# Score product of a neighbourhood attention: one strided matmul or two contiguous ones

## The chip, the cores and the metric

The kernel runs on 1 core of one Trainium2 chip. The metric is the device time of one execution in microseconds (us); the median of the runs is compared. The engines are named as in the profile: PE is the tensor engine's matmul, PEld its weight load, DVE the vector engine, ACT the scalar engine, POOL GpSimd, SP the engine that issues most transfers.

## What is computed

Two layers of a diffusion backbone over 512 latent tokens (a grid of 8 rows and 64 columns) and 256 context tokens, with 1024 features. Layer 1 mixes tokens in two ways, side by side: C, a neighbourhood attention with 8 heads of 64, and D, a bidirectional RWKV-7 recurrence. The change touches C alone:

```python
def neighborhood_attention(q, k, v, kc, vc, rpb):
    ...
    def block(args):
        ...
        s_loc = jnp.einsum('bchd,bicjhd->bhcij', q_row, ks, ...) * SCALE + bias
        s_ctx = jnp.einsum('bchd,bnhd->bhcn', q_row, kc, ...) * SCALE
        s = jnp.concatenate([s_loc.reshape(B, H, GRID_W, n_loc), s_ctx], axis=-1)
        p = jax.nn.softmax(s, axis=-1).astype(v.dtype)
        ...
        return (jnp.einsum('bhcij,bicjhd->bchd', p_loc, vs)
                + jnp.einsum('bhcn,bnhd->bchd', p[..., n_loc:], vc))
```

Every query sees a window of latent keys (8 rows by 16 columns) with a bias, and all 256 context keys, under one softmax.

## The kernel before, in words

The latent tokens of C are stored column by column of the grid (8 tokens to a column), so the window of 128 queries lies within 256 neighbouring keys. The heads are worked in 4 pairs (`odd_pair`), each pair in 4 blocks of 128 queries, each block once for each of the two heads u: 32 calls of the inner `attend(i, b, u, sums)`. One call takes a bank of PSUM `s` (tile `ps_a`, two buffers) of 128 queries by 512 keys: 256 near keys, which begin at token `START[b]`, and the 256 context keys. In the key tile `kt` (`ck` in the profile) each head has 768 columns, 512 latent ones and then the context. The near keys and the context are therefore two runs of 256 columns, at a distance of `NX - START[b]`. For block 3, whose near keys start at 256, that distance is 256, and the two runs are one.

Float32 precision of the scores is made with two products, j = 0 and 1: queries and keys are split into a high and a low part, stacked over the partitions, and the two matmuls (weights `qt[:, j, u, ...]`, tile `cq`) add up in PSUM. This is L1043, 64 matmuls in all. Then DVE adds the bias and takes the maximum (L1048, which reads the whole bank), ACT takes the exponential (L1049), four transposes (L1055) and their copy (L1057) follow, and the value product (L633) of the block after that; a division by the sums (L618, L622, L626) ends a pair.

These steps are generators laid piecewise among the steps of D's scan over the latent chunks (`rwkv_step`: matmuls L1307, L1313, L1326, L1336 and L1345, with 32 or 64 rows or columns of the array, copies L1317, L1329 and L1347, state updates L1337, L1340 and L1341), L3 = 1.7 pieces beside each. Beyond that, a scheduler sets the order on every engine, one instruction at a time, by priority and by when its operands are expected. Score products are written under `tc.high_priority(offset=QK_AHEAD)` with QK_AHEAD = 30, so they are placed ahead of what is written before them. Each engine then runs its own list in order, and waits on semaphores for the others.

## Time and profile before

| | |
|---|---|
| Median of 3 runs | 2101.39 us (2100.31 to 2101.66) |
| Span of the profiled execution | 2097.7 us, first to last instruction |
| Median less that span | 3.7 us |
| PE busy | 1990.2 us, 95% of the span, 15774 matmuls |
| DVE, ACT, POOL busy | 1229.5, 893.1, 232.8 us |
| Mean granted PE clock | 0.969 |
| Score matmuls L1043 | 64, from 1524.2 to 1648.6 us |

The profile is of one execution; its own time beside the span is not listed, so the span is held against the median of the runs. A row of a group reads: line, engine, operation, the tile written, the tiles read, shapes, count. In the order of time a row has the start, the length and the count of what was merged. A matmul in 32-bit float of the scan or of the value product stands with two records for each instruction; a score matmul and a transpose stand with one.

### The profile page before, as it was taken

How to read it: one execution, taken by the hardware profiler on the slowest of the kernel's cores; microseconds unless marked ns; L12 is line 12 of the kernel's file. 1: busy time of each engine (PE TensorE's matmuls, PEld its weight loads, DVE VectorE, ACT ScalarE, POOL GpSimd, SP SyncE). 2: the span in 40 equal slices, each digit the busy share in tenths (PEclk: the TensorE clock that was granted, in tenths of full speed). 3: DMA queues.
4: the chain of work that ended last, by engine and by line, in shares of the span. 5: the costliest groups of instructions: out<-in, count | busy, mean ns of one | idle time of the engine just before them, and what ended most of it. 6: DMA issues, size and time to landing. Idle time of an engine off the chain costs nothing.

```text
span 2097.7 us, 38650 instructions
## 1 busy us (share of the span) xinstructions
PE 1990.2 (95%) x15774; PEld 1619.9 (77%) x15774; DVE 1229.5 (59%) x2407; ACT 893.1 (43%) x1682; POOL 232.8 (11%) x346
## 2 busy tenths in 40 slices
PE   6999999999998999999999999889899989999997
PEld 4766788999987888787777776667667778888887
DVE  5756677666666443558445656786766774333335
ACT  3335567676733433552222345535245443222222
POOL 1111100000000010000112132322222120000000
PEclk9999999999999999999999899989789999999999
DMA  7363322433484444433434323356765133232321
GB/s 271 116 207 122 142 92 81 141 131 122 138 278 150 150 156 155 134 109 102 139 111 132 111 71 91 115 160 174 169 208 142 33 121 100 92 101 90 100 92 49
DMA packets 112656, 272.68 MB, mean 130 GB/s; under 512 B 15424, under 2 KB 48736, under 8 KB 110944
## 3 DMA queue, kind: packets, MB, share of 16 engines
q1 hardware_dynamic: 100256, 224.74, 33.8%
q0 software_dynamic: 12224, 45.49, 6.6%
q8 instruction: 124, 2.03, 0.4%
q14 instruction: 52, 0.43, 0.1%
HBM read 238.20 MB, written 31.98 MB: 129 GB/s over the span
## 4 chain that ended last, share of the span: by engine, by line
PE 46%; DVE 9%; issue 2%; ACT 2%; POOL 0%; DMA 0%; DVEq 0%; ACTq 0%
PE ps_b L385 10%; PE ps_b L386 10%; PE ps_b L387 10%; PE ps_w L1307 2%; PE ps_w L1313 1%; PE ps_s L1336 1%; DVE pi L1255 1%; PE ps_w L1326 1%; DVE kb L1251 1%; DVE kb L1258 1%; PE ps_a L1043 1%; PE ps_e L1214 1%; PE ps_w L1345 1%; PE ps_e L1055 1%; PE ps_v L633 1%
## 5 line engine op out<-in xcount | busy, mean ns | idle before, releaser
L143 ACT CAST whi<-wraw 128x1024 fp32r<-128x1024 f32 (+2 forms) x291 | 293.0, 1008 | 677.1 <-PE ps_b L386 513.7
L145 DVE TENSOR_TENSOR wlo<-wraw,whi 128x1024 fp32r<-128x1024 f32 (+2 forms) x251 | 296.4, 1181 | 217.8 <-ACT whi L143 211.2
L385 PE MATMUL ps_b<-hxh,whi 128*128 128x512 f32 (+1 forms) x1040 | 402.6, 390 | 13.2 <-ACT cj L974 7.2
L386 PE MATMUL ps_b<-hxl,whi 128*128 128x512 f32 (+1 forms) x1040 | 399.3, 386 | 0.8 <-DVE hxl L378 0.6
L387 PE MATMUL ps_b<-hxh,wlo 128*128 128x512 f32 (+1 forms) x1040 | 398.2, 385 | 0.8 <-POOL wlo L145 0.5
L385 PEld LDWEIGHTS ps_b<-hxh,whi 128*128 128x128 f32 x1040 | 199.0, 193 | 61.9 <-ACT cj L974 7.8
L386 PEld LDWEIGHTS ps_b<-hxl,whi 128*128 128x128 f32 x1040 | 199.7, 193 | 39.8 <-DVE hxl L378 2.2
L387 PEld LDWEIGHTS ps_b<-hxh,wlo 128*128 128x128 f32 x1040 | 199.6, 193 | 39.4 <-DVE wlo L145 1.4
L385 PE MATMUL ps_b<-act,whi 128*128 128x512 f32 (+1 forms) x570 | 199.9, 351 | 4.8 <-DVE xx L418 2.1
L387 PE MATMUL ps_b<-act,wlo 128*128 128x512 f32 (+1 forms) x570 | 196.6, 345 | 1.5 <-DVE wlo L145 1.5
L386 PE MATMUL ps_b<-act,whi 128*128 128x512 f32 (+1 forms) x570 | 196.0, 344 | 0.6 <-DVE act L124 0.6
L385 PE MATMUL ps_b<-hch,whi 128*128 128x256 f32 x552 | 159.4, 289 | 0.1
L387 PE MATMUL ps_b<-hch,wlo 128*128 128x256 f32 x552 | 155.8, 283 | 0.2 <-DVE wlo L145 0.2
L386 PE MATMUL ps_b<-hcl,whi 128*128 128x256 f32 x552 | 155.5, 282 | 0.0
L385 PEld LDWEIGHTS ps_b<-act,whi 128*128 128x128 f32 x570 | 109.0, 191 | 22.9 <-issue 6.8
L387 PEld LDWEIGHTS ps_b<-act,wlo 128*128 128x128 f32 x570 | 109.0, 191 | 14.9 <-DVE wlo L145 2.1
L386 PEld LDWEIGHTS ps_b<-act,whi 128*128 128x128 f32 x570 | 109.0, 191 | 12.9 <-DVE act L124 1.0
L418 DVE SCALAR_TENSOR_TENSOR xx<-ps_b,mod,xx 128x512 f32<-128x512 f32 (+1 forms) x64 | 43.7, 683 | 124.1 <-PE ps_b L387 123.5
L145 POOL TENSOR_TENSOR wlo<-wraw,whi 128x1024 fp32r<-128x1024 f32 (+1 forms) x40 | 88.2, 2212 | 205.4 <-ACT whi L143 198.6
L709 DVE TENSOR_TENSOR ff_a<-ff_a,ps_b 128x512 f32<-128x512 f32 x44 | 30.2, 686 | 134.5 <-PE ps_b L387 133.8
L385 PEld LDWEIGHTS ps_b<-hch,whi 128*128 128x128 f32 x552 | 104.1, 189 | 6.3 <-issue 2.6
L387 PEld LDWEIGHTS ps_b<-hch,wlo 128*128 128x128 f32 x552 | 104.1, 189 | 1.5 <-DVE wlo L145 1.0
(369 smaller groups left out, 3471.6 us busy)
## 6 DMA issues: line engine op xcount, KB each, us to landing
wraw<-in_ffi SPq DMA_DIRECT2D x132, 512.0 KB, 3.5
xx<-in_wmod POOLq DMA_DIRECT2D x48, 512.0 KB, 5.2
wraw<-in_w1in SPq DMA_DIRECT2D x43, 512.0 KB, 3.5
wraw<-in_ffo SPq DMA_DIRECT2D x48, 448.0 KB, 3.3
wmod<-in_wmod POOLq DMA_DIRECT2D x32, 512.0 KB, 4.7
wraw<-in_ffo SPq DMA_DIRECT2D x24, 512.0 KB, 3.5
op<-op SPq DMA_DIRECT2D x32, 384.0 KB, 3.9
qx<-in_wmod SPq DMA_DIRECT2D x16, 512.0 KB, 6.2
```

The source lines that it names most:

```text
L143: self.nc.scalar.copy(hi[:, 0:n], raw)
L145: e.tensor_tensor(lo[:, 0:n], raw, hi[:, 0:n].bitcast(F32), op=ALU.subtract)
L385: mm(out, lhsT=wh, rhs=hh, start=first, stop=False)
L386: mm(out, lhsT=wh, rhs=hl, start=False, stop=False)
L387: mm(out, lhsT=wl, rhs=hh, start=False, stop=last)
L418: self.nc.vector.scalar_tensor_tensor(X[:, m, c], ps[:, 0:n][:, c], gate[:, m, i : i + 1], X[:, m, c], op0=ALU.mult, op1=ALU.add)
L633: self.nc.tensor.matmul(ps[HD * u : HD * u + HD, col : col + P], lhsT=vs[u][j], rhs=pts[u][:, j, :], start=j == 0, stop=j == nk - 1, tile_ ...
L709: V.tensor_tensor(a, a, pg[1][:, 0:w], op=ALU.mult)
L1043: nc.tensor.matmul(s, lhsT=qt[:, j, u, P * b : P * b + P], rhs=k, start=j == 0, stop=j == 1)
L1055: nc.tensor.transpose(pt[:, P * j : P * j + P], p[:, P * j : P * j + P], self.ident)
L1214: nc.tensor.matmul(pg[r, c, 0:W], lhsT=KB[r, c, :], rhs=AR[r, c, :], start=True, stop=True)
L1307: mm(wy[HD * u + HD - W_ + r : HD * u + HD, p, :], lhsT=G[top[u], p, r:W_], rhs=VU[top[u], p, u, :], start=p == 0, stop=False, skip_group_ ...
```

## The change

The one matmul of 512 columns with a stride between two runs becomes two of 256 contiguous columns, near and context, each summed over j on its own half of the bank. The order of writing is near j = 0, near j = 1, context j = 0, context j = 1. All else that differs between the two files is comments and docstrings; lines below move by two (L1048 is L1050 in the changed kernel, L1307 is L1309, and so on).

```diff
         def attend(i, b, u, sums):
             s = self.bank("a")
-            c, d = NT * u + START[b], NX - START[b]
-            k = kt[:, c : c + 2 * d].rearrange("p (a n) -> p a n", a=2)[:, :, 0:256]
+            near, ctx = (kt[:, c : c + 256] for c in (NT * u + START[b], NT * u + NX))
             with self.tc.high_priority(offset=QK_AHEAD):
-                for j in range(2):
-                    nc.tensor.matmul(s, lhsT=qt[:, j, u, P * b : P * b + P], rhs=k, start=j == 0, stop=j == 1)
+                for i, k in enumerate((near, ctx)):
+                    for j in range(2):
+                        nc.tensor.matmul(
+                            s[:, 256 * i : 256 * i + 256], lhsT=qt[:, j, u, P * b : P * b + P], rhs=k, start=j == 0, stop=j == 1
+                        )
             v = (1, 0, 0, 2)[b]
```

PE's order in the scan step beside the second pair of heads, query block 2, head 1 (`ps_a_16316`), before. `ps_w` is the scan's PSUM, `VU`, `op` and `Sd` its operands:

```order
L1313 MATMUL ps_w_16263<-Sd_1521_7227,op_2809_16044 64x64 x8
L1043 MATMUL ps_a_16316<-ck_15848,cq_15847 128x512
L1307 MATMUL ps_w_16282<-VU_1527_7237,op_2810_16048 64x64
L1043 MATMUL ps_a_16316<-ck_15848,cq_15847 128x512
L1307 MATMUL ps_w_16282<-VU_1527_7237,op_2810_16048 64x64
L1307 MATMUL ps_w_16282<-VU_1527_7237,op_2810_16048 32x64 x6
L1313 MATMUL ps_w_16282<-Sd_1525_7235,op_2810_16048 64x64 x8
```

The score product breaks into the scan's L1307 at two places. The same place in the changed kernel:

```order
L1315 MATMUL ps_w_16289<-Sd_1521_7227,op_2809_16060 64x64 x8
L1043 MATMUL ps_a_16342<-ck_15858,cq_15857 128x256
L1309 MATMUL ps_w_16308<-VU_1527_7237,op_2810_16064 64x64
L1043 MATMUL ps_a_16342<-ck_15858,cq_15857 128x256
L1309 MATMUL ps_w_16308<-VU_1527_7237,op_2810_16064 64x64
L1043 MATMUL ps_a_16342<-ck_15858,cq_15857 128x256
L1309 MATMUL ps_w_16308<-VU_1527_7237,op_2810_16064 32x64
L1043 MATMUL ps_a_16342<-ck_15858,cq_15857 128x256
L1309 MATMUL ps_w_16308<-VU_1527_7237,op_2810_16064 32x64 x5
L1315 MATMUL ps_w_16308<-Sd_1525_7235,op_2810_16064 64x64 x8
```

Now there are four places, with a scan matmul between each two. A little later, PE's order around the last block of the same pair (block 3, head 1, `ps_a_16372`), before:

```order
L1326 MATMUL ps_w_16263<-W_16280,op_2809_16044 32x64 x8
L1043 MATMUL ps_a_16372<-ck_15848,cq_15847 128x512
L1326 MATMUL ps_w_16282<-W_16299,op_2810_16048 32x64
L1043 MATMUL ps_a_16372<-ck_15848,cq_15847 128x512
L1326 MATMUL ps_w_16282<-W_16299,op_2810_16048 32x64 x7
```

There the second matmul follows one scan matmul after the first. The same place in the changed kernel:

```order
L1328 MATMUL ps_w_16308<-W_16325,op_2810_16064 32x64
L1043 MATMUL ps_a_16402<-ck_15858,cq_15857 128x256
L1328 MATMUL ps_w_16308<-W_16325,op_2810_16064 32x64
L1043 MATMUL ps_a_16402<-ck_15858,cq_15857 128x256
L1328 MATMUL ps_w_16308<-W_16325,op_2810_16064 32x64
L1043 MATMUL ps_a_16402<-ck_15858,cq_15857 128x256
L1328 MATMUL ps_w_16308<-W_16325,op_2810_16064 32x64
L1043 MATMUL ps_a_16402<-ck_15858,cq_15857 128x256
L1328 MATMUL ps_w_16308<-W_16325,op_2810_16064 32x64 x4
```

Again four single matmuls take the place of two. Over the whole program the score matmuls stand in 50 uninterrupted runs before, and in 81 after.

## The prediction

> **What bounds the kernel now.** I read the page first (engines and the chain that ended last), then the rows of the changed line, the stretch in which that line runs, and last the order of time on the tensor engine (PE) there.

> ```profile
> span 2097.7 us, 38650 instructions
> PE 1990.2 (95%) x15774; PEld 1619.9 (77%) x15774; DVE 1229.5 (59%) x2407; ACT 893.1 (43%) x1682; POOL 232.8 (11%) x346
> PE 46%; DVE 9%; issue 2%; ACT 2%; POOL 0%; DMA 0%; DVEq 0%; ACTq 0%
> ```

> PE is the busiest engine and by far the largest engine in the chain. Matmuls are pipelined, so a busy share alone proves little; the next rows narrow it to the place of the change.

> ```profile
> L1043 PE MATMUL ps_a<-ck,cq x64: 387/498/797, 1524.2 to 1648.6; 128*128 128x512 f32 x64
> 1523.00:1560.00 37.00, 32.12 (x446) 23.61 (x444) 25.78 (x49) 15.95 (x41) 10.00 (x20) 0.81 0.59 187
> 1540.00:1650.00 110.00, 109.48 (x1636) 79.41 (x1635) 71.85 (x158) 56.57 (x138) 24.61 (x42) 1.00 0.47 134
> PE ps_v L633 <- DVE hxh L1057: 0.3, 2, 0.2
> ```

> The 64 score matmuls of the C attention run from 1524 to 1649 us, and nowhere else. The second and third rows give busy time of PE, weight loads, DVE, ACT and POOL, then the granted clock and the DMA share. From 1540 to 1650 us PE is busy 109.48 of 110 us at clock 1.00, while DVE has 71.85 and ACT 56.57. The last row is the only wait of PE's matmuls in that stretch, 0.3 us. What is added to PE's queue there has no hole of its own to go into; what is taken off DVE or ACT there gains nothing.

> **What one score matmul costs, where it stands now.** The attention is laced into the RWKV scan, whose matmuls (L1307 to L1345) use 32 or 64 rows or columns of the array. A score matmul (128*128) thus often stands alone among small ones. Two such places, in order of time (start, length, and "x14" counts two records for each scan instruction):

> ```profile
> 1579.79 0.50 PE L1043 MATMUL ps_a<-ck,cq 128*128 128x512 f32 x1
> 1580.22 0.32 PE L1307 MATMUL ps_w<-VU,op 32*64 32x64 f32 x2
> 1580.47 0.49 PE L1043 MATMUL ps_a<-ck,cq 128*128 128x512 f32 x1
> 1580.90 0.78 PE L1307 MATMUL ps_w<-VU,op 32*64 32x64 f32 x14
> 1581.60 0.69 PE L1313 MATMUL ps_w<-Sd,op 128*64 128x64 f32 x16
> ...
> 1585.75 0.49 PE L1043 MATMUL ps_a<-ck,cq 128*128 128x512 f32 x1
> 1586.18 0.29 PE L1326 MATMUL ps_w<-W,op 32*32 32x64 f32 x2
> 1586.40 0.51 PE L1043 MATMUL ps_a<-ck,cq 128*128 128x512 f32 x1
> 1586.84 0.63 PE L1326 MATMUL ps_w<-W,op 32*32 32x64 f32 x14
> 1587.40 0.66 PE L1055 MATMUL ps_e<-ident,hxl 128*128 128x128 f32 x4
> ```

> I go by starts, not lengths, because lengths overlap. From 1580.22 to 1580.90 PE does one scan instruction and one score matmul: 0.68 us. A scan instruction in a run of its own takes 0.70 / 7 = 0.10 us (1580.90 to 1581.60). One visit of a lone score matmul therefore costs 0.58 us. At the second place: 1586.18 to 1586.84 is 0.66, less 0.56 / 7 = 0.08, again 0.58. The same 512 columns cost far less in a run of full matmuls:

> ```profile
> 1104.34 0.39 PE L385 MATMUL ps_b<-hxh,whi 128*128 128x512 f32 x1
> 1104.57 0.39 PE L386 MATMUL ps_b<-hxl,whi 128*128 128x512 f32 x1
> 1104.80 0.39 PE L387 MATMUL ps_b<-hxh,wlo 128*128 128x512 f32 x1
> 1105.11 1.08 PE L1326 MATMUL ps_w<-W,op 32*32 32x64 f32 x32
> ...
> 1182.74 0.28 PE L385 MATMUL ps_b<-act,whi 128*128 128x256 f32 x1
> 1182.86 0.28 PE L386 MATMUL ps_b<-act,whi 128*128 128x256 f32 x1
> 1182.98 0.28 PE L387 MATMUL ps_b<-act,wlo 128*128 128x256 f32 x1
> 1183.19 0.52 PE L1326 MATMUL ps_w<-W,op 32*32 32x64 f32 x12
> ...
> 371.62 0.44 PE L633 MATMUL ps_v<-sm_t,vt 128*64 128x128 f32 x4
> 371.99 0.38 PE L385 MATMUL ps_b<-hch,whi 128*128 128x256 f32 x1
> 372.21 0.28 PE L386 MATMUL ps_b<-hcl,whi 128*128 128x256 f32 x1
> 372.33 0.29 PE L387 MATMUL ps_b<-hch,wlo 128*128 128x256 f32 x1
> ```

> In a run, 512 columns take 0.23 us and 256 columns 0.12, each with its own weight load. So a visit pays 0.58 - 0.23 = 0.35 us for going from small tiles to the full array and back. That part does not shrink with the columns: leaving to L1326 takes 0.31 us after 512 columns (1104.80 to 1105.11) and 0.21 after 256 (1182.98 to 1183.19), only the 0.10 of the columns less; and the first 256-column matmul after small tiles takes 0.22 (371.99 to 372.21) where the next takes 0.12.

> **The change, part by part.**

> *More instructions.* 64 matmuls of 512 columns become 128 of 256, and 64 weight loads become 128. Columns and sums are the same. Standing in a run, two halves cost 2 x 0.12 instead of 0.23: 0.01 us more for each of 64, 0.6 us.

> *More visits.* This is the main term. The scheduler places matmuls one by one, so the halves are laced into the scan separately, as the two pieces of the order show. I counted the uninterrupted runs of score matmuls in both orders: 50 before (40 of them a single matmul), 81 after (67 single). 31 more visits at 0.35 us are 10.9 us.

> *Bounds of a visit's price.* Low: only the way out as the settled rows show it, 0.31 - 0.23 = 0.08, gives 31 x 0.08 + 0.6 = 3.1 us. High: a visit among the value matmuls:

> ```profile
> 1584.03 0.43 PE L633 MATMUL ps_v<-hxh,cv 128*64 128x128 f32 x2
> 1584.39 0.49 PE L1043 MATMUL ps_a<-ck,cq 128*128 128x512 f32 x1
> 1584.82 0.44 PE L633 MATMUL ps_v<-hxh,cv 128*64 128x128 f32 x4
> ```

> 1584.03 to 1584.82 is 0.79; less one value matmul (at most 0.11) and 0.23 it leaves 0.45, so 31 x 0.45 + 0.6 = 14.6 us. I take 0.35, since 23 of the 31 new visits have L1307 or L1326 on both sides, where it was measured (visits of that kind go from 20 to 43 by the orders).

> *The first score matmuls.* They sit before a stall, and there the added work is free:

> ```profile
> 1525.37 7.69 DVE L1263 STREAM_TRANSPOSE G<-kb 32x1024 f32<-32x1024 f32 x4
> 1528.66 0.80 PE L1043 MATMUL ps_a<-ck,cq 128*128 128x512 f32 x1
> 1534.33 1.19 PE L1043 MATMUL ps_a<-ck,cq 128*128 128x512 f32 x2 [4.87 <-DVE sm_m L1048]
> ```

> PE waits 4.87 us for a bank of ps_a that DVE reads only after its four transposes. DVE's order is the same here in both kernels, and the third block's scores stand behind the second's in both, so the stall stays and eats the four extra matmuls ahead of it. They are four back to back, so this is under 0.1 us and I leave it in.

> *What could cover the rest.* PE's idle time from 1540 to 1650 us is 110 - 109.48 = 0.5 us; I subtract all of it.

> *The other engines.* DVE reads a whole bank (L1048) as before; it gets a block's scores one or two visits later, but has 38 us of slack in the 110. A few DVE and ACT copies swap neighbours (VU copies against L1048 and the copies L1057), and on SP an operand load of the scan and a weight load change places; with DMA at 0.47 and no DMA among PE's waits I cost these at nothing. If that cover is gone, the scan's next step (L1307) would be late, on the same PE queue.

> *Sum.* 10.9 + 0.6 - 0.5 = 11.0 us. The work after 1650 us follows in PE's order, so the end moves with it. The profiled span goes from 2097.7 to 2108.7; the median of the runs, 2101.39, is 3.7 above that span for what lies around it, so I expect 2112.4.

> [...]

> **The rivals.**

> *No measurable change (within 0.2%, about 4.2 us, which is what a measurement of this kernel can tell).* The pieces' extra visits would have to hide behind scan latency (PE to ACT to PE), or the loads be pulled ahead at the changes of tile too. For it: the scan is a chain across engines, and modelled ends may make a waiting PE look busy. Against it: 0.5 us idle in 110 and the same visit price at two places. At the low end of 0.08 a visit: 3.1 us, 2104.5.

> *Half of it hides.* Visits that end at an L1307 or L1336 which waits anyway would cost nothing more. If half of 10.9 goes: 5.5 + 0.6 = 6.1, 2107.5.

> *Faster: contiguous columns stream faster.* Before, near keys and context are two runs with a step between them; if PE paid for that, every score matmul would gain. It would have to be over (11.0 + 4.2) / 64 = 0.24 us for each, more than the 0.23 that 512 contiguous columns take at all. The trace has its own control: query block 3 starts at key 256, so there the two runs are already one of 512. The matmuls at 1585.75 and 1586.40 are of block 3, those at 1579.79 and 1580.47 of block 2 with a gap. From score matmul to the next small one: 0.43 and 0.44 against 0.43 and 0.43. There is nothing to gain; were it 0.25 us, the time would be 2101.4 + 11.0 - 16.0 = 2096.4.

> [...]

> **How the numbers follow.** Full price of the visits (2109.5 to 2116): 0.73. Half hidden (2105.6 to 2109.5): 0.13. No measurable change: 0.10, taken as within 0.2%. Faster: 0.04. The first two are both slower, 0.86. The predicted time is that of the first. For 8 in 10 the range takes in the first case and most of the second: 2106 to 2116; the upper end is the price among value matmuls, 2101.4 + 14.6.

> **What would show it.** After: 128 rows of L1043 with 256 columns and 15838 matmuls in all; singles whose start to the next small one is about 0.32 instead of 0.43; back to back about 0.12; the stretch from the stall's end to the last score matmul some 11 us longer, with PE still busy all along; nothing changed ahead of 1524 us, and all after 1660 shifted as a block. I am wrong if PE shows new idle time there (a wait took over), if a single 256-column visit costs 0.3 rather than 0.47, or if the clock in 1523 to 1560 us (0.81) falls further, which adds on top.

## The result, and the profile after

The changed kernel takes 2125.62 us (median of 4 runs, 2122.62 to 2128.73) against 2100.85 us before (4 runs, 2100.17 to 2101.66): ratio 1.0115, 95% interval 1.0099 to 1.0132, so 24.8 us slower. The direction was forecast; the size was 11.0 us and the range ended at 2116. The profiled execution has a span of 2126.7 us.

From the page of the changed kernel: the span, the engines, and the chain that ended last by engine.

```profile
span 2126.7 us, 38780 instructions
PE 2015.9 (95%) x15838; PEld 1643.4 (77%) x15838; DVE 1230.5 (58%) x2407; ACT 893.3 (42%) x1682; POOL 232.7 (11%) x346
PE 47%; DVE 9%; issue 2%; ACT 1%; POOL 0%; DMA 0%; DVEq 0%; ACTq 0%
```

64 matmuls more, as written, and nothing new in the chain. The rows of the score matmuls and of who waits for them, then the stretches from 1523 to 1560 and from 1540 to 1650 us (busy time of PE, weight loads, DVE, ACT, POOL, then the granted clock, DMA share and GB/s), one that reaches to the last score matmul (PE, clock, DMA, GB/s), and the only wait of PE's matmuls in it:

```profile
L1043 PE MATMUL ps_a<-ck,cq x128: 278/384/582, 1526.9 to 1677.1; 128*128 128x256 f32 x128
  DVE sm_m L1050: 4.9, 1
  DVE hxl L1050: 34.0, 19
...
1523.00:1560.00 37.00, 32.05 (x429) 25.42 (x426) 24.36 (x47) 14.40 (x36) 9.22 (x18) 0.74 0.52 174
1540.00:1650.00 110.00, 109.80 (x1410) 82.53 (x1408) 60.98 (x134) 46.57 (x113) 23.37 (x40) 0.90 0.50 142
...
1560.00:1677.00 117.00, 116.81 (x1383) 0.87 0.39 104
...
PE ps_v L633 <- DVE hxh L1059: 0.2, 1, 0.2
```

The stretch of score matmuls has grown from 124.4 us (1524.2 to 1648.6) to 150.2 (1526.9 to 1677.1), 25.8 us. That is nearly all of the 29.0 us by which the two profiled spans differ; it starts 2.7 us later, and the profiled execution is the slowest of the four, 3.1 us above their median. PE is as full as before. What is new is one column: the granted clock, 1.00 before, is 0.90 in the same 110 us and 0.87 from 1560 to 1677 us. The kernel before, over that last stretch, and its row of who waits for the scores:

```profile
1560.00:1677.00 117.00, 116.33 (x1490) 1.00 0.38 106
...
  DVE hxl L1048: 17.9, 14
```

In the records of both profiled runs the clock is 1.0 or 0.5 and nothing between (34 stretches before, 46 after), so a mean of 0.87 over 117 us is 2 x 0.13 x 117 = 30.4 us at half speed, where there was none. Other runs show it too. The time at half speed over a whole run is 2 x (1 - mean clock) x span: 157 to 170 us in the four runs of the changed kernel, 164 on average, and 122 to 151 us in the 29 runs of the kernel before that were taken beside the first four experiments, 137 on average (162 and 130 in the two profiled runs).

The order of time shows the two losses next to each other:

```profile
1607.58 0.38 PE L1043 MATMUL ps_a<-ck,cq 128*128 128x256 f32 x1
1607.89 0.32 PE L1309 MATMUL ps_w<-VU,op 32*64 32x64 f32 x2
1608.14 0.38 PE L1043 MATMUL ps_a<-ck,cq 128*128 128x256 f32 x1
1608.45 0.29 PE L1309 MATMUL ps_w<-VU,op 32*32 32x64 f32 x2
1608.68 0.38 PE L1043 MATMUL ps_a<-ck,cq 128*128 128x256 f32 x1
1608.99 0.41 PE L1309 MATMUL ps_w<-VU,op 32*32 32x64 f32 x6
1609.33 0.38 PE L1043 MATMUL ps_a<-ck,cq 128*128 128x256 f32 x1
1609.64 0.29 PE L1309 MATMUL ps_w<-VU,op 32*32 32x64 f32 x2
1609.87 0.38 PE L1043 MATMUL ps_a<-ck,cq 128*128 128x256 f32 x1
1610.18 0.29 PE L1309 MATMUL ps_w<-VU,op 32*32 32x64 f32 x2
1610.40 0.38 PE L1043 MATMUL ps_a<-ck,cq 128*128 128x256 f32 x1
1610.72 0.48 PE L1315 MATMUL ps_w<-Sd,op 128*64 128x64 f32 x2
1611.12 0.58 PE L1043 MATMUL ps_a<-ck,cq 128*128 128x256 f32 x1
1611.64 1.01 PE L1315 MATMUL ps_w<-Sd,op 128*64 128x64 f32 x13
...
1604.10:1607.50 3.40, 3.40 (x54) 1.00 1.05 377
1607.50:1610.90 3.40, 3.40 (x24) 0.97 1.02 190
1610.90:1614.30 3.40, 3.40 (x35) 0.53 1.01 195
```

Seven visits in a row. In six of them 0.31 or 0.32 us pass from the score matmul to the next small one; in the seventh, at half clock, 0.52. In the stretch of 3.4 us from 1607.50 only 24 matmuls start, against 54 in the one ahead of it, though PE counts as busy throughout. Right behind it the clock is halved (0.53 over the next 3.4 us): the scan's L1315 takes 1.01 us for 13 records, where 16 took 0.69 in the kernel before.

### The profile page after: what moved, and what is told of

It is laid out like the page before. It is cut to its first block, busy times and chain, and to the rows that moved or that the text cites. A ratio compares the mean times of both kernels' runs of the same rounds, so it can differ in the third digit from the quotient of the medians.

```text
span 2126.7 us, 38780 instructions
## 1 busy us (share of the span) xinstructions
PE 2015.9 (95%) x15838; PEld 1643.4 (77%) x15838; DVE 1230.5 (58%) x2407; ACT 893.3 (42%) x1682; POOL 232.7 (11%) x346
## 4 chain that ended last, share of the span: by engine, by line
PE 47%; DVE 9%; issue 2%; ACT 1%; POOL 0%; DMA 0%; DVEq 0%; ACTq 0%
PE ps_b L385 10%; PE ps_b L386 10%; PE ps_b L387 10%; PE ps_w L1309 2%; PE ps_w L1315 2%; PE ps_a L1043 1%; PE ps_s L1338 1%; DVE pi L1257 1%; PE ps_w L1328 1%; DVE kb L1253 1%; DVE kb L1260 1%; PE ps_e L1057 1%; PE ps_v L633 1%; PE ps_e L1216 1%; PE ps_w L1347 1%
## 5 line engine op out<-in xcount | busy, mean ns | idle before, releaser
L385 PE MATMUL ps_b<-hxh,whi 128*128 128x512 f32 (+1 forms) x1040 | 402.5, 390 | 12.9 <-ACT cj L974 7.1
L386 PE MATMUL ps_b<-hxl,whi 128*128 128x512 f32 (+1 forms) x1040 | 399.0, 386 | 0.9 <-DVE hxl L378 0.7
L387 PE MATMUL ps_b<-hxh,wlo 128*128 128x512 f32 (+1 forms) x1040 | 397.4, 384 | 0.8 <-POOL wlo L145 0.6
L385 PEld LDWEIGHTS ps_b<-hxh,whi 128*128 128x128 f32 x1040 | 198.7, 192 | 61.7 <-ACT cj L974 7.8
L386 PEld LDWEIGHTS ps_b<-hxl,whi 128*128 128x128 f32 x1040 | 199.3, 192 | 40.0 <-DVE hxl L378 2.4
L387 PEld LDWEIGHTS ps_b<-hxh,wlo 128*128 128x128 f32 x1040 | 199.2, 192 | 39.5 <-DVE wlo L145 1.3
L385 PE MATMUL ps_b<-act,whi 128*128 128x512 f32 (+1 forms) x570 | 200.0, 351 | 5.2 <-DVE xx L418 2.1
L387 PE MATMUL ps_b<-act,wlo 128*128 128x512 f32 (+1 forms) x570 | 196.5, 345 | 1.5 <-DVE wlo L145 1.5
L386 PE MATMUL ps_b<-act,whi 128*128 128x512 f32 (+1 forms) x570 | 195.9, 344 | 0.6 <-DVE act L124 0.6
L385 PE MATMUL ps_b<-hch,whi 128*128 128x256 f32 x552 | 159.4, 289 | 0.1
L387 PE MATMUL ps_b<-hch,wlo 128*128 128x256 f32 x552 | 155.9, 283 | 0.2 <-DVE wlo L145 0.2
L386 PE MATMUL ps_b<-hcl,whi 128*128 128x256 f32 x552 | 155.5, 282 | 0.0
L385 PEld LDWEIGHTS ps_b<-act,whi 128*128 128x128 f32 x570 | 108.9, 191 | 23.2 <-issue 6.8
L387 PEld LDWEIGHTS ps_b<-act,wlo 128*128 128x128 f32 x570 | 108.9, 191 | 15.0 <-DVE wlo L145 2.1
L386 PEld LDWEIGHTS ps_b<-act,whi 128*128 128x128 f32 x570 | 109.1, 191 | 13.0 <-DVE act L124 1.0
L385 PEld LDWEIGHTS ps_b<-hch,whi 128*128 128x128 f32 x552 | 104.2, 189 | 6.3 <-issue 2.6
L387 PEld LDWEIGHTS ps_b<-hch,wlo 128*128 128x128 f32 x552 | 104.0, 189 | 1.5 <-DVE wlo L145 1.0
```

Source lines behind the costliest of these rows:

```text
L385: mm(out, lhsT=wh, rhs=hh, start=first, stop=False)
L386: mm(out, lhsT=wh, rhs=hl, start=False, stop=False)
L387: mm(out, lhsT=wl, rhs=hh, start=False, stop=last)
```

## The experiments

All are set against the kernel before, run on the same chip. Its median beside the first four was 2101.95 us, beside the last two 2102.67.

**Contiguity alone.** One matmul of 512 as before, on contiguous columns (blocks 0 to 2 leave out the context and read the 256 columns behind the near keys); the order on every engine is the old one.

```diff
-            c, d = NT * u + START[b], NX - START[b]
-            k = kt[:, c : c + 2 * d].rearrange("p (a n) -> p a n", a=2)[:, :, 0:256]
+            c = NT * u + START[b]
+            k = kt[:, c : c + 512] if b < 3 else kt[:, NT * u + 256 : NT * u + 768]
```

> One matmul of 512 as before, but its 512 key columns are contiguous for every block (for blocks 0 to 2 the wrong keys: near keys and the 256 columns behind them instead of the context). The order on every engine is that of the kernel before. Theory (the step between the two runs costs nothing): within 2 us of before. Rival (contiguous columns stream faster): up to 48 matmuls gain, so 5 to 12 us faster than before.

Measured: 2101.61 us, ratio 0.9997 (0.9987 to 1.0008). The step between the runs costs nothing that can be measured; the faster rival is out, as the rows of block 3 had said.

**The split, its four matmuls left together.** Against the changed kernel:

```diff
-            with self.tc.high_priority(offset=QK_AHEAD):
+            with self.tc.high_priority(offset=200):
```

> The changed kernel with the scores' priority offset 200 instead of 30, which makes the scheduler leave the four matmuls of a block together: 30 runs of score matmuls instead of 81 (50 before). Theory (the loss is the visits among small tiles, and a clock that falls because the lone matmuls leave the array less busy): PE needs 50 - 30 = 20 visits x 0.35 = 7.0 us less than before, less 0.6 us for the halves and what the other neighbours cost: 2 to 7 us faster than before, with the granted clock at 1.00 between 1560 and 1650 us. Rival 1 (the split itself costs, whatever stands between): still 10 us or more slower than before. Rival 2 (the earlier scores make DVE or the scan late): slower than before with PE idle in that stretch.

Measured: 2097.82 us, ratio 0.9982 (0.9968 to 0.9995), 4.1 us faster than before and 28 us faster than the changed kernel by the medians, with the same 128 matmuls of 256. From its trace: the score rows, a visit, the stretch from 1540 us, and the scan's last matmul group.

```profile
L1043 PE MATMUL ps_a<-ck,cq x128: 274/282/582, 1524.4 to 1638.0; 128*128 128x256 f32 x128
  DVE hxl L1050: 0.6, 2
...
1586.20 0.74 PE L1043 MATMUL ps_a<-ck,cq 128*128 128x256 f32 x4
1586.87 0.43 PE L633 MATMUL ps_v<-hxh,cv 128*64 128x128 f32 x2
...
1540.00:1650.00 110.00, 109.99 (x1786) 88.33 (x1784) 73.67 (x170) 59.94 (x146) 23.47 (x42) 1.00 0.50 137
...
L1347 PE MATMUL ps_w<-VU,op x512: 214/219/316, 1410.8 to 1650.4; 128*32 128x64 f32 x128, 32*32 32x64 f32 x43
```

Four halves take 0.67 us together (1586.20 to 1586.87); lone ones cost some 0.46 each in the changed kernel. PE starts 1786 matmuls in the 110 us in which the changed kernel starts 1410, and the clock is 1.00. Rival 1 falls: the split by itself does not cost 10 us. Rival 2 falls too: DVE's wait for scores shrinks from 34.0 to 0.6 us. The last score matmul starts 10.6 us earlier than before (1638.0 against 1648.6), but the scan, which now has more left behind it, ends only 3.6 us earlier: its last matmul starts at 1650.4, before at 1654.0.

```profile
L1345 PE MATMUL ps_w<-VU,op x512: 214/219/316, 1412.5 to 1654.0; 128*32 128x64 f32 x128, 32*32 32x64 f32 x43
```

**One matmul of 512, left together.** The same offset of 200, on the kernel before:

> The kernel before with the priority offset 200: one matmul of 512 for each j as before, in 29 runs instead of 50. Theory: 21 visits x 0.35 = 7.4 us less work for PE, priced pair by pair from the spacings of before 5.3 us: 3 to 8 us faster than before, and 0 to 3 us faster than the split with the same offset. Rival (the placement of the scores on PE does not matter, the scan's chain sets the time): within 2 us of before.

Measured: 2094.45 us, ratio 0.9971 (0.9961 to 0.9981), 7.5 us faster by the medians. It beats both kernels. Against the split with the same offset it is 3.4 us faster by the medians, just outside the 0 to 3 expected; the two intervals overlap, so the price of the halves in a run is not settled between 0.6 and some 3 us. Its stretch, with clock 1.00 and more matmuls started than before (1710 against 1636):

```profile
1540.00:1650.00 110.00, 109.23 (x1710) 82.36 (x1705) 77.71 (x174) 59.45 (x141) 25.35 (x44) 1.00 0.48 126
```

**Visits without the slow clock.** Against the kernel before:

```diff
-                for j in range(2):
-                    nc.tensor.matmul(s, lhsT=..., rhs=k, start=j == 0, stop=j == 1)
+                for n in range(4):
+                    j = n % 2
+                    nc.tensor.matmul(s, lhsT=..., rhs=k, start=n == 0, stop=n == 3)
```

> Four matmuls of 512 columns for each block and head instead of two (each product is added twice, so the scores come out doubled). The scheduler puts them in 99 runs, more than the 81 of the changed kernel, and PE streams twice its columns. At full clock that is 49 visits x 0.35 = 17.2 us and 64 x 0.23 = 14.7 us over before, pair by pair 27.4 us. Theory (the changed kernel lost some 13 us more than its visits because the clock is halved where full-height streaming falls under some 0.31 of a 3.4 us window, and wider matmuls keep it above): 25 to 33 us over before, that is little more than the changed kernel's 25, with at most two half-clock windows between the first 1560 us and the last score matmul. Rival (the clock falls with the number of lone matmuls or weight loads): more half-clock windows than the changed kernel, 40 us or more over before.

Measured: 2130.38 us, ratio 1.0140 (1.0125 to 1.0154), 28.4 us over before. PE streams twice the score columns of the changed kernel in 18 more visits, and is only 4.8 us slower than it by the medians.

```profile
L1044 PE MATMUL ps_a<-ck,cq x128: 387/502/796, 1525.5 to 1678.4; 128*128 128x512 f32 x128
...
1560.00:1677.00 117.00, 117.00 (x1386) 0.99 0.39 104
```

The clock holds at 0.99, one half-clock stretch of 3.4 us in the records. The rival fails: with more lone matmuls than the changed kernel (88 single ones against 67) and as many weight loads (128 in both), the clock did not drop. The full-clock sum, 27.4 us pair by pair (each gap between two starts at the price of that pair of matmuls before), is nearly all of the 28.4; at 0.35 us a visit it would be 31.9, so that price is too high for some of these 49 visits.

**The split, not contiguous.** Against the kernel before, in place of the same two lines:

```diff
+                for n in range(4):
+                    i, j = n // 2, n % 2
+                    q = slice(128 * i, 128 * i + 128)
+                    nc.tensor.matmul(
+                        s.rearrange("p (a n) -> p a n", a=2)[:, :, q], lhsT=..., rhs=k[:, :, q], start=j == 0, stop=j == 1,
+                    )
```

> The split without the contiguity: each of the two matmuls takes 128 near columns and 128 context columns, a strided pair of runs on the key side and on the PSUM side. The scheduler puts the scores in 81 runs, as in the changed kernel. Theory (only visits and the clock count): as the changed kernel, 22 to 28 us over before, with about six half-clock windows between 1560 us and the last score matmul. Rival (contiguity is worth something that the split hid): 5 us or more slower than the changed kernel.

Measured: 2126.08 us, ratio 1.0129 (1.0096 to 1.0162), 23.4 us over before by the medians (one of its four runs took 2135.44, which lifts the ratio): as the changed kernel. There are five half-clock stretches after 1560 us. Contiguity made no difference that these runs can tell, on either side of the matmul; the interval spans some 14 us, so e1 is the sharper evidence for the key side.

**Half of the split.** Against the kernel before, in place of the same two lines:

```diff
+                for n in range(2 * u + 2):
+                    i, j = n // 2, n % 2
+                    o, r = (s, k) if u == 0 else (s[:, 256 * i : 256 * i + 256], k[:, i, :])
+                    nc.tensor.matmul(o, lhsT=..., rhs=r, start=j == 0, stop=j == 1)
```

> Only the second head of each pair (u = 1) is split; the first keeps its matmuls of 512. 96 score matmuls in 67 runs: 17 visits more than before, where the changed kernel has 31. Theory: visits 17 x 0.35 + 32 x 0.01 = 6.3 us (5.4 pair by pair), and windows in which full-height streaming falls under 0.31 in some three places against five in the changed kernel, at about 2.4 us for each: 10 to 16 us over before in all, with two to four half-clock stretches between 1560 us and the last score matmul. Rival (the visits alone, the clock an accident of the changed kernel): 5 to 7 us over before and no half-clock stretch there.

Measured: 2112.80 us, ratio 1.0052 (1.0036 to 1.0068), 10.1 us over before, at the low end of what was expected, and more than the visits' 6.3 alone. There are three half-clock stretches of 3.4 us after 1560 us. The stretch of 117 us in the last two, e5 first and then this one:

```profile
1560.00:1677.00 117.00, 116.76 (x1445) 0.90 0.38 102
...
1560.00:1677.00 117.00, 116.74 (x1481) 0.96 0.38 103
```

Two terms come near all four slow kernels: the added matmuls at full clock, and half of the time at half clock (which is the clock's deficit times 117 us). Changed kernel: 11.5 + 15.2 = 26.7, measured 24.8. Four full ones: 27.4 + 1.2 = 28.6, measured 28.4. Strided split: 11.5 + 11.7 = 23.2, measured 23.4. One head: 6.3 + 4.7 = 11.0, measured 10.1. The sum for the four full ones is priced pair by pair, the others by the visit, and the clock is that of one execution against a median of several: what is shown is agreement within some 3 us, not better.

## Why the prediction was wrong, point by point

- **The visit's price was right.** A lone score matmul of 256 was to cost 0.47 us. From 1608.45 to 1608.99 PE does one L1309 and one visit: 0.54 us, less 0.08 for the scan instruction is 0.46. From score to small matmul it was to be 0.32 us and is 0.31. 31 more visits at this price give about the 10.9 us they were given.
- **Where they hide: nowhere, as said.** PE's idle time in the 110 us went from 0.5 to 0.2 us, so at most 0.3 of the 0.5 that was subtracted was to be had. The stall ahead of the third block stayed (4.9 us, DVE's L1050).
- **The step that failed is the sum.** It ran all of 1540 to 1650 us at clock 1.00, because the kernel before shows 1.00 there, and left the clock to the last sentence, without a price, and only for 1523 to 1560 us. The missing term is the 30.4 us at half clock behind 1560 us, worth some 13 to 15 us: more than the term that was worked out. To check that sum, I priced every gap from one PE matmul's start to the next, between the first and the last score matmul, by the median of the same pair at full clock before (where a pair is new, that of the 512-column one less 256 columns). Gaps that begin at half clock exceed their price by 23.2 us after and 8.8 before (the stall included), 14.4 us more. That leaves 11.4 of the 25.8 us for everything at full clock, and 10.9 + 0.6 = 11.5 had been forecast for it. The clocks of all runs say the same: 164 less 137 is 27 us more at half speed, of which half is lost, 13 us. The sign that the forecast did name came as well, and is small: from 1523 to 1560 us the clock is 0.74, not 0.81.
- **The range could not hold it.** Its upper end was the dearest visit at full clock. A term that multiplies everything in the stretch was not among the unknown costs.
- **The rivals.** Contiguous columns: no effect, as the two blocks' rows had it. The half-hidden visits and the loads that are pulled ahead: excluded by the four-full kernel. With half of its 17.2 us of visits hidden it would have been 8.6 + 14.7 + 1.2 = 24.5 us over before (visits, columns, clock), and its interval begins at 26.3. As to the loads: in a run of full tiles before, one starts some 0.2 us ahead of its matmul (L387's at 1104.57, the matmul at 1104.80); at the change of tile the two start together (L1043's at 1580.47 before, and at 1608.68 in the changed kernel).
- **Other engines.** DVE's wait for scores doubled from 17.9 to 34.0 us. It had PE to wait for, and no wait of PE for DVE grew, so no cost of its own is to be seen.

## What to carry to other kernels

Count a new matmul not by its columns but by what stands on each side of it in PE's order: alone among matmuls of small tiles it paid 0.35 us besides its columns, in a run of full tiles 0.01. When a change makes a saturated PE stream less in each microsecond, price the clock as well: here 30.4 of 117 us passed at half clock, and that slowed all that ran there, the scan included (L1315 took 1.01 us for 13 records, where 16 had taken 0.69). And where a scheduler laces work into other work, its order is worth a knob: raising one priority offset from 30 to 200 left the same matmuls together and made the kernel 7.5 us faster than the starting point.

## What the runs showed of the hardware

This is a pattern over windows. The four-full kernel is the one run that keeps the lone visits and raises the share, so the test rests on it. The pattern has exceptions: 26 windows under 0.31 had no halving behind them, one of 0.29 in the changed kernel's stretch (from 1593.6 us) among them, and the four-full kernel's one halving there followed a window of 0.35. Without the weighting by rows the two groups separate nearly as well over the whole programs (at 0.38), but not in this stretch, where the six windows then lie between 0.32 and 0.49. What the chip counts stays open.
